# Attention on one core: eight pairs instead of ten transposed by transfers, another order of groups, a warm-up of 24 short matmuls, and stores split late

## The chip, the core and the metric

The kernel runs on one core of a Trainium2 chip. The core has five engines that run side by side and wait for each other by semaphores: TensorE (PE; its weight loads are listed as PEld), VectorE (DVE), ScalarE (ACT), GpSimd (POOL) and SyncE (SP). SyncE and ScalarE issue the DMAs here; 16 DMA engines carry them out. The metric is the device time of one execution in microseconds.

## The reference

Plain softmax attention for 8 batches of 8 heads, 512 positions of 64 values each:

```python
def reference(q, k, v):
    scale = 1.0 / np.sqrt(q.shape[-1])
    scores = np.einsum('bhqd,bhkd->bhqk', q, k) * scale
    scores = scores - scores.max(axis=-1, keepdims=True)
    attn = np.exp(scores)
    attn = attn / attn.sum(axis=-1, keepdims=True)
    return np.einsum('bhqk,bhkd->bhqd', attn, v).astype(np.float32)
```

The kernel leaves the maximum out, takes exp(scores x scale) as it is, and gets the sum of each row as a 65th output column, from a column of ones beside v.

## The kernel before

**Work.** The 64 heads are 32 pairs, g = 0 to 31. Of a pair, the 512 keys are four blocks of 128 (c = 0 to 3), each for two heads: 8 blocks of 128 keys x 512 queries, 256 in all. Two blocks make a group, m, with one exponential of 128 x 1024; there are 128 groups and four to a pair (the last group is split into two halves). Three buffers of the accumulation memory hold scores, so the scores of group m wait until the exponential of an earlier group has read its buffer.

**Steps of a pair.** Three loads bring q, k and v in 32 bits (`load`). GpSimd converts them to 16 bits (`cast`): q and k into `qkp`, v into one of 12 tiles `vp`. q and k must be transposed into `tqk`. For most pairs TensorE does so (`transposes`, 8 matmuls against an identity, and `copy`, one VectorE copy of 128 x 1024). For the pairs in `FLIPPED` a transposing DMA does so, from `qkp` to `tqk` without TensorE and VectorE (`flip`). Then come the scores (`scores`, two matmuls per group, one for each head, on separate halves of the rows), the exponential, and the output (`values`: for each 128 queries of a head, called a unit, four matmuls of 65 columns accumulate over the key blocks). Seven units share one bank of the accumulation memory; VectorE takes the reciprocals of their sums and multiplies (`recip`, `norm`, `mult`) into a ring of 56 units, from which SyncE stores (`Stores`). There are two such banks (`x0`, `x1`), which the transposes use too.

**Who exponentiates.** ScalarE does 115 groups. For the 13 groups in `ON_DVE`, VectorE computes the exponential by a polynomial: TensorE first adds a constant by two matmuls (`lift`), then VectorE runs `raise_` and three passes over 128 x 1024. For the groups in `SHARED`, GpSimd computes the middle one of the three. In most of them the scores' buffer is free after the second pass; in those of `SHARED` and `FREED` it is after the first.

**Order.** `Plan` walks through a model of the kernel in steps of 5 ns, with a cost for each kind of step, and writes a list of steps; the kernel then issues the instructions in the order of that list, and each engine takes its own in that order. So a constant of `Plan` moves no work by itself: it changes where in each engine's queue a step stands. `LATE_NORM`, `LATE_MULT` and `LATE_COPY` say how long a ready normalisation or copy may be held back for a pass; `ROOM` when a normalisation is taken in two parts; `SLACK` how far behind a VectorE group's last pass its block counts as there. A DMA in SyncE's queue waits for its data, and for the landing of an earlier DMA whose semaphore it reuses; everything behind it waits too.

**Stores.** `Stores.ready` gives a store of both heads of a pair (256 KB) where they lie side by side in the ring, and of one head (128 KB) otherwise. The last head is apart: its output comes in two halves of two units (`last_values`, `finish`), the first stored by SyncE, the second by ScalarE's queue.

**Start.** Pair 0 is written out by hand (`first_pair`): TensorE multiplies ones by ones (`busy`) until q is there, then transposes in pieces, with more such matmuls in the gaps, and the first three groups go through four exponentials (L846). The others are L650.

Of the kernel before, what the change touches and what calls it, by code (L numbers as in the profile page):

```python
# [16 lines left out]

class Stores:

    def __init__(self, pairs, units):  # L20
        self.pairs, self.units = pairs, units
        self.started = []
        self.waiting = []
# [5 lines left out]
    def ready(self, upto):  # L29

        found = []
        while self.waiting and self.waiting[0][2] + 4 <= upto:
            g, h, u = self.waiting[0]
            n = 1
            if h == 0 and u % self.units + 8 <= self.units:
                if len(self.waiting) > 1:
                    if self.waiting[1][0] == g:
                        n = 2
                elif g < self.pairs - 1 and (g, 1 - h) not in self.started:
                    break  # L40
            if u + 4 * n > upto:
                break
            found.append(self.waiting[:n])
            del self.waiting[:n]
        return found

class Plan:
# [7 lines left out]
    COPY_1 = (400, 190)  # L56
    NORM_COLUMN, PASS_DONE = 67, 80
    RECIP, RECIP_DONE, CHAINED = 80, 230, 117
    APART, ROOM = 1, 1200
    PASS, PASSES = 1131, 3  # L60
    OFFSET = 216
    FIRST_EXP = 5130
    STEP = 5
    CALM, KEEN = 14000, 7
    FIRST_UNIT, FIRST_VALUES = 4, 6000
    ON_DVE = (8, 16, 29, 36, 48, 53, 65, 74, 82, 90, 97, 104, 112)
    SHARED = (48, 90, 104)
    FREED = (36, 97, 112)

    LATE_NORM, LATE_MULT, LATE_COPY, HURRY, SOON, BACKLOG = 1000, 1300, 1000, 800, 80, 1500  # L70
    SLACK, AHEAD = 300, 2

    CAST, CAST_DONE, TO_POOL = 560, 130, 150
    SCALED, MORE = 595, 75
    MIDDLE, MIDDLE_DONE = (1120, 2300), 250
    FIRST_LAND, LOAD, STORE, LATENCY, ISSUE, FLIP_ISSUE = 5200, 700, 350, 2300, 540, 1490
    RAW, QK16, NV = 7, 5, 12
    FLIPPED = (22, 23, 24, 25, 26, 27, 28, 29, 30, 31)
    LEAD, FLIP = 8000, 3500
    RING = 56  # L80

    def __init__(self, groups, pairs, first):
# [27 lines left out]

        late = {grp[0][0] for m, grp in enumerate(groups) if m in self.ON_DVE}
        due = []
        for g in range(pairs):
            scores = 5000 + 3380 * g
            if g:
                lead = self.LEAD if g in self.FLIPPED else 2300
                due += [(scores - lead, g, "k"), (scores - lead + 10, g, "q")]
# [3 lines left out]
        self.extra = {}  # L121
        for m in self.ON_DVE:
            g = groups[m][0][0]
# [15 lines left out]
    def released(self, m):  # L139
        return 0 if m in self.SHARED or m in self.FREED else 1  # L140

# [3 lines left out]
    def emit(self, t, after):  # L145
# [3 lines left out]
        if not shared:  # L149
            self.casts.append((g, n, t if after is None else after + self.TO_POOL))  # L150
        if n == "q" and g in self.FLIPPED:
            self.note(t, "flip", g)
# [65 lines left out]
    def for_dve(self, m):  # L218
        return m in self.ON_DVE

# [29 lines left out]
    def transposes(self, t):  # L250
# [6 lines left out]
        if self.part_t == 2:  # L257
            self.transposed[self.next_t] = self.pe + self.TO_DVE
            self.ready.append((self.pe + self.TO_DVE, "copy", (self.next_t, self.bank_t)))
            self.next_t += 1  # L260
            while self.next_t in self.FLIPPED:
                self.next_t += 1
# [92 lines left out]
    def step_dve(self, t):  # L355
# [56 lines left out]
        elif any(x[2] <= t for x in self.passes):  # L412
# [5 lines left out]
            if all(x[0] > end - late[x[1]] for x in self.ready):  # L418
# [11 lines left out]
                del self.passes[after]  # L430
                if s == 0 and m in self.SHARED:
                    self.passes.remove((m, 1, 1e9))
# [24 lines left out]
def kernel(  # L457
# [7 lines left out]
    nc = tc.nc  # L465
    B, H, S, D = q.shape
    P = 128
# [6 lines left out]
    LAST = NP - 1  # L474
# [11 lines left out]
    raises = {}  # L486
    for m in Plan.ON_DVE:
        (g, c, _), (g2, c2, _) = groups[m]
# [35 lines left out]
    def source(src, g):  # L524
        b, h = g // ppb, 2 * (g % ppb)
        return src[b, h : h + 2].rearrange("h (p i) d -> p h i d", i=NI)
# [151 lines left out]
    def pass_(m, s):  # L678
# [7 lines left out]
        last = s == 2  # L686
        shared = m in Plan.SHARED
        one = low if m not in Plan.FREED else f
        dve(
# [78 lines left out]
    def finish(half):  # L768
        o = last[half]
        n = slice(2 * half, 2 * half + 2)  # L770
        ob = opool.tile([P, 2, D], FP32, tag="obl", name=f"obl_{half}")
        rc = opool.tile([P, 7, 1], FP32, tag="rc", name=f"rc_last_{half}")
        nc.vector.reciprocal(out=rc[:, 0:2], in_=o[:, :, D : D + 1])  # L773
        nc.vector.tensor_tensor(  # L774
            out=ob[:, :, :],
            in0=o[:, :, 0:D],
            in1=rc[:, 0:2].broadcast_to([P, 2, D]),
            op=AluOp.mult,
        )
        queue = (nc.sync, nc.scalar)[half]  # L780
        queue.dma_start(out=source(out, LAST)[:, 1, n], in_=ob[:, :, :])

    def first_loads():
        tk = load_tile(0, "k")
# [11 lines left out]
    def busy(dst, n):  # L796

        nc.tensor.matmul(dst[:, 0:n], ones[:, 0:P], ones[:, 0:n], start=True, stop=True)  # L798

    def first_pair():  # L800

        tk, tq = raw[0]["k"], raw[0]["q"]
        k16 = cpool.tile([P, 2, NI, D], FP16, name="k16_0")
        q16 = cpool.tile([P, 2, NI, 2, D], FP16, name="q16_0")
        kt = cpool.tile([P, 2, 2, P], FP16, name="kt_0")
        qt = cpool.tile([P, 2, NI, P], FP16, name="qt_0")

        def twice(h, i, n):
            return tq[:, h, i : i + n].rearrange("p i (x d) -> p i x d", x=1).broadcast_to([P, n, 2, D])  # L810

        nc.vector.tensor_copy(out=q16[:, 0, 0:2], in_=twice(0, 0, 2))
        nc.vector.tensor_copy(out=k16[:, 0, 0:2], in_=tk[:, 0, 0:2])
        nc.vector.tensor_copy(out=q16[:, 0, 2:4], in_=twice(0, 2, 2))
        nc.scalar.copy(k16[:, 0, 2:4], tk[:, 0, 2:4])
        nc.gpsimd.tensor_copy(out=q16[:, 1, 0:2], in_=twice(1, 0, 2))
        nc.gpsimd.tensor_copy(out=k16[:, 1, 2:4], in_=tk[:, 1, 2:4])

        pka, st1, st0 = (buffer(b, f"st_{n}") for b, n in enumerate(("ka", "1", "0a")))
        pqa = ps_x.tile([P, 8, P], FP16, tag="x0", name="tp_qa")  # L820
        pqb = ps_x.tile([P, 8, P], FP16, tag="x1", name="tp_qb")

        pka, pkc, pqc = pka[:, 0, :], st1[:, 0, :], st1[:, 1, :]
        pka, pkc, pqc = (
            t.bitcast(FP16).rearrange("p (n c) -> p n c", c=P) for t in (pka, pkc, pqc)
        )

        def t_k(dst, h, j):
            nc.tensor.transpose(
                dst, k16[:, h, 2 * j : 2 * j + 2, :].rearrange("p i d -> p (i d)"), ident  # L830
            )

        def t_q(dst, h, i):
            nc.tensor.transpose(dst, q16[:, h, i].rearrange("p x d -> p (x d)"), ident)  # L834

        def first_scores(st, h, j, q0, q1, pt, s0, s1):
            for x in range(2):
                s = slice(64 * x, 64 * x + 64)
                nc.tensor.matmul(  # L839
                    st[:, x, s0:s1],  # L840
                    kt[s, h, j, :],
                    qt[s, h].rearrange("p i c -> p (i c)")[:, q0:q1],
                    start=True,
                    stop=True,
                )
            nc.scalar.activation(  # L846
                out=pt[:, :, q0:q1], in_=st[:, :, s0:s1], func=EXP, scale=scale
            )

        for n in (512, 512, 512, 512, 512, 256):  # L850
            busy(st0[:, 0], n)
        for i in range(2):
            t_q(pqa[:, i], 0, i)
        t_k(pka[:, 0], 0, 0)
        busy(st0[:, 0], 2 * P)
        for i in range(2):
            t_q(pqc[:, i], 0, 2 + i)
        t_k(pkc[:, 0], 0, 1)
        nc.vector.tensor_copy(out=qt[:, 0, 0:2], in_=pqa[:, 0:2])
        nc.vector.tensor_copy(out=kt[:, 0, 0], in_=pka[:, 0])  # L860
        nc.vector.tensor_copy(out=qt[:, 0, 2:4], in_=pqc[:, 0:2])
        nc.vector.tensor_copy(out=kt[:, 0, 1], in_=pkc[:, 0])
        nc.vector.tensor_copy(out=q16[:, 1, 2:4], in_=twice(1, 2, 2))
        nc.vector.tensor_copy(out=k16[:, 1, 0:2], in_=tk[:, 1, 0:2])
        busy(st0[:, 1], 2 * P)
        pts = [ppool.tile([P, 2, S], FP16, tag="pt", name=f"pt_{m}") for m in range(3)]
        for m in range(3):
            for x, b in enumerate(groups[m]):
                blocks[b] = pts[m][:, x, :]
        first_scores(st0, 0, 0, 0, 256, pts[0], 0, 256)  # L870
        st0b = buffer(0, "st_0b")
        busy(st0b[:, 0, 256:512], P)
        first_scores(st0b, 0, 0, 256, 512, pts[0], 0, 256)
        first_scores(st1, 0, 1, 0, S, pts[1], 0, S)
        for i in (2, 3, 0, 1):
            t_q(pqb[:, i], 1, i)
        nc.vector.tensor_copy(out=qt[:, 1], in_=pqb[:, 0:4])  # L877
        pkb = ps_x.tile([P, 8, P], FP16, tag="x0", name="tp_kb")
        for j in range(2):
            t_k(pkb[:, j], 1, j)  # L880
        nc.vector.tensor_copy(out=kt[:, 1, 0], in_=pkb[:, 0])
        st2 = buffer(2, "st_2")
        busy(st2[:, 0], 3 * P)
        first_scores(st2, 1, 0, 0, S, pts[2], 0, S)
        nc.vector.tensor_copy(out=kt[:, 1, 1], in_=pkb[:, 1])
        first.update(kt=kt, qt=qt)
# [64 lines left out]
```

## Time and profile before

| | |
|---|---|
| three timed runs | 119.07, 116.71, 116.79 us (median 116.79) |
| the profiled execution | 116.59 us, its span 114.8 us |
| TensorE, matmuls | busy 103.4 us (90%), 1500 |
| VectorE | busy 100.3 us (87%), 179 instructions |
| ScalarE | busy 107.4 us (94%), 119 |
| GpSimd | busy 73.3 us (64%), 121 |
| DMA | 36.43 MB, mean 317 GB/s; 379 to 386 GB/s in most slices up to 50 us |
| the chain that ended last | ScalarE 70%, TensorE 17% |

A line of the profile's groups names the source line, the engine, the operation, the tile written and the tiles read, how many, then busy time and mean ns of one, then the idle time of the engine just before them and what ended most of it. In the timeline and the chain a line begins with its start and its length in us; `x8` says that eight instructions are merged in it. The span counts from the first instruction of the program to the last; the time of an execution is longer by what the profile does not cover. An instruction's duration can hold time in which it stood in line behind the one before it, so the pace of a row of equal instructions is read from their starts.

VectorE's and TensorE's busy shares over stretches of the span, in us:

| stretch | TensorE | VectorE | ScalarE | GpSimd |
|---|---|---|---|---|
| 10 to 25 | 13.75 | 13.72 | 15.00 | 11.15 |
| 25 to 40 | 13.61 | 13.92 | 15.00 | 11.45 |
| 40 to 55 | 14.56 | 14.56 | 15.00 | 10.90 |
| 55 to 70 | 14.11 | 14.71 | 15.00 | 11.53 |
| 70 to 80 | 9.73 | 9.93 | 10.00 | 6.30 |
| 80 to 90 | 9.86 | 9.73 | 10.00 | 7.98 |
| 90 to 100 | 9.34 | 9.74 | 10.00 | 7.23 |
| 100 to 110 | 9.22 | 7.59 | 10.00 | 1.51 |

### The profile page before, as it was taken

The numbers are of one execution on the slowest core, as the hardware profiler recorded it, in microseconds if no ns is written. First come the engines' busy times: TensorE is split into PE (matmuls) and PEld (weight loads), VectorE is DVE, ScalarE is ACT, GpSimd is POOL, SyncE is SP. The second block draws the span as 40 slices with busy tenths as digits, with TensorE's granted clock in tenths as the row PEclk, the third lists the DMA queues.
The fourth block names the chain that finished last, engine by engine and source line by source line (L and its number), as shares of the span: only waits on it lengthen the run. The fifth ranks groups of instructions, "written<-read, shape, count | busy, mean of one in ns | idle before, by whom it ended". The sixth has DMA issues, their size and how long they took to land.

```text
span 114.8 us, 3911 instructions
## 1 busy us (share of the span) xinstructions
PE 103.4 (90%) x1500; PEld 63.4 (55%) x1500; DVE 100.3 (87%) x179; ACT 107.4 (94%) x119; POOL 73.3 (64%) x121
## 2 busy tenths in 40 slices
PE   7979999798998999999898999999999989979970
PEld 2435564465563565666564566555667555547650
DVE  4653799996999999999999999999999999997480
ACT  4399999999999999999999999999999999999970
POOL 2289845969995629994779496593995557922000
PEclk9999999999999999999999999999999999999999
DMA  3899999999999999999999999989999999997452
GB/s 97 265 367 380 384 379 380 386 379 379 383 382 381 377 384 385 374 383 381 357 364 379 375 285 332 313 252 352 226 320 327 135 332 329 197 339 244 135 184 90
DMA packets 45795, 36.43 MB, mean 317 GB/s; under 512 B 12752, under 2 KB 45776, under 8 KB 45776
## 3 DMA queue, kind: packets, MB, share of 16 engines
q1 hardware_dynamic: 45344, 35.86, 101.0%
q10 hardware_dynamic: 432, 0.33, 0.9%
q8 instruction: 11, 0.18, 0.6%
q14 instruction: 8, 0.07, 0.2%
HBM read 25.17 MB, written 8.39 MB: 292 GB/s over the span
## 4 chain that ended last, share of the span: by engine, by line
ACT 70%; PE 17%; issue 7%; DMA 2%; DVE 2%; ACTq 0%
ACT pt L650 69%; PE st L645 7%; PE o L743 6%; DMA q<-in_q_dram 2%; ACT pt L846 1%; PE st L839 1%; DVE obl L774 1%; PE st_0a L798 0%; DVE qt L877 0%; PE tp_qa L834 0%; DVE rc_last L773 0%; PE tp_qb L834 0%; PE tp L593 0%; PE st_0b L839 0%; PE st_0a L839 0%
## 5 line engine op out<-in xcount | busy, mean ns | idle before, releaser
L650 ACT ACTIVATE pt<-st 128x1024 f16<-128x1024 f32 (+1 forms) x113 | 102.8, 1204 | 0.0
L645 PE MATMUL st<-tqk 64*128 64x512 f16 (+1 forms) x250 | 47.5, 380 | 6.1 <-ACT pt L650 4.6
L743 PE MATMUL o<-vp,pt 128*128 128x65 f16 x904 | 44.6, 195 | 0.2 <-ACT pt L650 0.2
L743 PEld LDWEIGHTS <-pt 128*128 128x128 f16 x904 | 36.2, 98 | 15.6 <-issue 14.4
L551 POOL CAST vp<-v 128x512 f16<-128x512 f32 x32 | 19.6, 619 | 8.8 <-PE o L743 2.4
L645 PEld LDWEIGHTS <-tqk 64*128 64x128 f16 x250 | 14.1, 93 | 17.8 <-issue 9.3
L568 POOL CAST qkp<-k 128x512 f16<-128x512 f32 x31 | 19.0, 614 | 7.0 <-DVE y L690 1.7
L719 DVE TENSOR_TENSOR ring<-o,rc 128x448 f32<-128x448 f32 (+2 forms) x37 | 22.4, 607 | 0.8
L568 POOL CAST qkp<-q 128x512 f16<-128x512 f32 x30 | 18.5, 616 | 6.8 <-DVE pd L690 2.9
L668 DVE TENSOR_SCALAR z<-st 128x1024 f32<-128x1024 f32 x13 | 15.7, 1206 | 0.9 <-PE st L645 0.9
L743 PE MATMUL o<-vp,pd 128*128 128x65 f16 x104 | 16.2, 195 | 0.1
L690 DVE SCALAR_TENSOR_TENSOR pd<-y,z 128x1024 uint32<-128x1024 f32 x13 | 16.0, 1229 | 0.0
L690 DVE SCALAR_TENSOR_TENSOR y<-st,z 128x1024 f32<-128x1024 uint16 x13 | 15.6, 1203 | 0.1
L613 DVE COPY tqk<-tp 128x1024 f16<-128x1024 f16 x20 | 13.6, 680 | 2.1 <-PE tp L593 1.9
L593 PE MATMUL tp<-ident,qkp 128*128 128x128 f16 x168 | 13.7, 220 | 0.1
L593 PEld LDWEIGHTS <-qkp 128*128 128x128 f16 x168 | 9.6, 98 | 5.8 <-issue 3.2
L743 PEld LDWEIGHTS <-pd 128*128 128x128 f16 x104 | 10.2, 98 | 3.0 <-issue 2.6
L711 DVE RECIPROCAL rc<-o 128x7 f32<-128x7 f32 (+2 forms) x37 | 7.3, 197 | 3.8 <-PE o L743 3.6
L567 POOL TENSOR_SCALAR k<-k 128x128 f32<-128x128 f32 x13 | 6.9, 530 | 4.4 <-PE st L645 2.6
L690 DVE SCALAR_TENSOR_TENSOR y<-st,y 128x1024 f32<-128x1024 uint16 x7 | 8.5, 1208 | 0.0
L706 POOL TENSOR_TENSOR y<-t,y 128x1024 f32<-128x1024 f32 x3 | 7.1, 2369 | 0.2
L631 PE MATMUL st<-const-bfloat16-1.0,lift 64*128 64x512 bf16 x26 | 5.0, 379 | 0.0
(57 smaller groups left out, 34.4 us busy)
## 6 DMA issues: line engine op xcount, KB each, us to landing
v<-in_v_dram SPq DMA_DIRECT2D x32, 256.0 KB, 5.4
k<-in_k_dram SPq DMA_DIRECT2D x31, 256.0 KB, 5.4
q<-in_q_dram SPq DMA_DIRECT2D x31, 256.0 KB, 5.4
out_dram<-ring SPq DMA_DIRECT2D x27, 256.0 KB, 4.4
out_dram<-ring SPq DMA_DIRECT2D x9, 128.0 KB, 4.3
tqk<-qkp SPq DMA_TRANSPOSE x10, 5.3
k<-in_k_dram ACTq DMA_DIRECT2D x1, 128.0 KB, 2.6
q<-in_q_dram SPq DMA_DIRECT2D x2, 64.0 KB, 2.3
```

The source lines that it names most:

```text
L551: return nc.gpsimd.tensor_copy(out=vps[g % NV][:, :, :, 0:D], in_=raw[g]["v"][:, :, :, :])
L568: ins = nc.gpsimd.tensor_copy(out=dst, in_=src[:, :, :, :])
L593: nc.tensor.transpose(tps[g][:, n, i, :], qkp[g][:, n, i, :], ident)
L613: nc.vector.tensor_copy(out=tqk[g][:, :, :], in_=tps.pop(g).rearrange("p n i c -> p n (i c)"))
L645: nc.tensor.matmul(st[:, x, cols], kc, qc[:, cols], start=not on_dve, stop=True)
L650: nc.scalar.activation(out=pt[:, :, cols], in_=st[:, :, cols], func=EXP, scale=scale)
L668: nc.vector.tensor_scalar(out=r["z"][:, :, :], in0=r["st"][:, :, :], scalar1=128.0, scalar2=2.0**17, op0=AluOp.mult, op1=AluOp.max,)
L690: nc.vector.scalar_tensor_tensor(out=r["bits"][:, :, :] if last else y, in0=(low, one, y)[s], scalar=(QUARTIC if shared else CUBIC)[s], in ...
L706: nc.gpsimd.tensor_tensor(out=y[:, :, :], in0=t[:, :, :], in1=y[:, :, :], op=AluOp.mult)
L711: dve(nc.vector.reciprocal(out=rcs[u][:, 0:n], in_=o[:, x : x + n, D : D + 1]))
L719: nc.vector.tensor_tensor(out=ring[:, u % NU : u % NU + n, :], in0=o[:, x : x + n, 0:D], in1=rc[:, 0:n].broadcast_to([P, n, D]), op=AluOp. ...
L743: nc.tensor.matmul(os[u // 7][:, u % 7, :], blocks[(g, c, h)][:, y * P : (y + 1) * P], vps[g % NV][:, h, c, :], start=(c == 0), stop=(c == ...
```

## The change

Pairs 22 and 23 are transposed by TensorE and not by a transfer. The 13 groups of VectorE are others (three of them shared with GpSimd as before, two instead of three in `FREED`), and four limits of the planner change; with them the order of nearly every engine changes from about group 18 on. From pair 25 on, the two heads of a pair are stored apart. Each of the last two stores is issued as two halves of 64 partitions, one on SyncE's queue and one on ScalarE's. The matmuls of ones at the start are cut into pieces of 128 columns: 24 first (five of 512 and one of 256 before), then 2, 2, 1 and 3 for 256, 256, 128 and 384 columns. There are 152 DMAs in place of 147: two transposing ones less, five stores of the ring and two of the last head more.

```diff
 class Stores:
+    MERGED = 25
...
-            if h == 0 and u % self.units + 8 <= self.units:
+            if h == 0 and g < self.MERGED and u % self.units + 8 <= self.units:
...
-    APART, ROOM = 1, 1200
+    APART, ROOM = 1, 2500
...
-    ON_DVE = (8, 16, 29, 36, 48, 53, 65, 74, 82, 90, 97, 104, 112)
-    SHARED = (48, 90, 104)
-    FREED = (36, 97, 112)
-
-    LATE_NORM, LATE_MULT, LATE_COPY, HURRY, SOON, BACKLOG = 1000, 1300, 1000, 800, 80, 1500
-    SLACK, AHEAD = 300, 2
+    ON_DVE = (8, 16, 26, 36, 44, 50, 62, 70, 79, 85, 96, 103, 111)
+    SHARED = (44, 79, 96)
+    FREED = (85, 103)
+
+    LATE_NORM, LATE_MULT, LATE_COPY, HURRY, SOON, BACKLOG = 1600, 1300, 2200, 800, 80, 1500
+    SLACK, AHEAD = 100, 2
...
-    FLIPPED = (22, 23, 24, 25, 26, 27, 28, 29, 30, 31)
+    FLIPPED = (24, 25, 26, 27, 28, 29, 30, 31)
...
-        queue = (nc.sync, nc.scalar)[half]
-        queue.dma_start(out=source(out, LAST)[:, 1, n], in_=ob[:, :, :])
+        for x, queue in enumerate((nc.sync, nc.scalar)):
+            some = slice(64 * x, 64 * x + 64)
+            queue.dma_start(out=source(out, LAST)[some, 1, n], in_=ob[some, :, :])
...
-        for n in (512, 512, 512, 512, 512, 256):
-            busy(st0[:, 0], n)
+        for _ in range(24):
+            busy(st0[:, 0], P)
...
-        busy(st0[:, 0], 2 * P)
+        for n in range(2):
+            busy(st0[:, 0], P)
...
-        busy(st0[:, 1], 2 * P)
+        for n in range(2):
+            busy(st0[:, 1], P)
...
-        busy(st0b[:, 0, 256:512], P)
+        for n in range(1):
+            busy(st0b[:, 0, 256:512], P)
...
-        busy(st2[:, 0], 3 * P)
+        for n in range(3):
+            busy(st2[:, 0], P)
```

## The prediction

> **What bounds the kernel now.** I read the groups of instructions first, then the list for the line of the exponentials, the chain of waits at both ends, and the timeline of the DMA queue.
>
> ```profile
> L650 ACT ACTIVATE pt<-st 128x1024 f16<-128x1024 f32 (+1 forms) x113 | 102.8, 1204 | 0.0
> ...
> L650 ACT ACTIVATE pt<-st x113: 722/1227/1321, 8.3 to 110.4; 128x1024 f16<-128x1024 f32 x111, 128x512 f16<-128x512 f32 x2
> ```
>
> The last column of the first line is ScalarE's idle time before these instructions: 0.0. The second gives first and last start. Between them lie 111 full exponentials and one half, so (110.4 - 8.3 - 0.5) / 111 = 0.915 us for each (0.5: the half, which the chain starts at 109.95). I call 0.915 us a slot. ScalarE never waits for 102 us, so nothing that is sped up in the middle can show; only work ahead of 8.3 us, work behind the last exponential, or a new hole in ScalarE's row can.
>
> ```profile
> 3.46 0.40 PE tp_qa L834 x2
> ...
> 3.97 0.21 PE st_0a L798
> 4.18 0.21 PE st L834 x2
> ...
> 6.00 0.34 PE tp_qb L834 x4
> 6.34 0.03 issue
> 6.37 0.42 DVE qt L877
> 6.79 0.14 DVE kt L881
> 6.93 0.05 issue
> 6.98 0.41 PE st L839 x2
> 7.38 0.02 issue
> 7.41 1.02 ACT pt L846
> 8.43 24.33 ACT pt L650 x27
> ```
>
> Start, length, what: the chain before the steady state starts when the first q and its cast are there (3.46) and runs over TensorE, VectorE, TensorE. Two matmuls of 128 columns take 0.21 us at 4.18; the eight of one tile at 7.51 take 0.62 from first start to last end, 0.22 being one alone, so 0.057 each. TensorE goes at half pace until shortly before 5.9 us, though the page's clock row shows 9 throughout. The fourth exponential starts 0.27 us after ScalarE fell idle.
>
> ```profile
> 110.72 0.31 PE o_last L759 x4
> ...
> 111.75 0.29 DVE obl L774
> ...
> 112.08 0.35 ACTq L781 DMA_DIRECT2D out_dram<-obl  x1
> ```
>
> The tail: the last store is issued at 112.08 and SyncE waits 1.7 us for its landing (until 113.7); 1.1 us of closing work follows.
>
> ```profile
> 85.88 1.39 SPq L599 DMA_TRANSPOSE tqk<-qkp  x1
> ...
> 96.05 2.51 SPq L599 DMA_TRANSPOSE tqk<-qkp  x1
> ...
> 99.29 1.28 SPq L599 DMA_TRANSPOSE tqk<-qkp  x1
> ...
> DMA to landing us min/median/max: 3.3/5.3/6.5
> ```
>
> These transposing transfers (pairs 27, 30, 31; the last line is over all ten) are the one supply with little to spare. The scores of pair 27 begin on TensorE at 92.81, 6.9 us behind the issue; of pair 30 at 102.51, 6.5 behind; of pair 31 at 106.52, 7.2 behind. At the median landing, 1.2 to 1.9 us are over.
>
> **The change part by part.** The sum is made against the profiled execution: 116.59 us, a span of 114.8 and 1.8 around it. The three timed runs have 116.71, 116.79 and 119.07, so it stands 0.2 below their median.
>
> *Warm-up.* Out go five matmuls of 512 columns and one of 256 (2,816 columns, 0.76 to 3.06 at 0.427 us per 512); in come 24 of 128 (3,072 columns). At 0.107 each, the pace of the cold 128-column matmuls, 24 take 2.56 us and end their streaming at 3.32, ahead of 3.46, when the first q is ready. Cover 0.14 us, cost 0. That each loads its own weights (0.147 us, the median of that line) costs nothing where loads overlap: the transposes at 3.97 to 4.29 each load their own and still come every 0.107. The other splits (two, two, one and three of 128) keep their columns. I take 0; the ends are +3.4 and -0.6, both rivals below.
>
> The Trainium skill, "TensorE: Matmul & The Clock Gate", section "Part 3: Packing small matmuls", says that a weight load overlaps running matmuls only if it is for another row group. By that rule 24 loads at the page's 107 ns would stand in line with 24 matmuls, 5.1 us instead of 2.56. This trace disagrees: full-height transposes, one row group, come every 0.107 us with a load each.
>
> *Two more pairs transposed on TensorE* (22 and 23): 16 matmuls of 0.057, 0.9 us, and two copies of 0.68 on VectorE, 1.36 us. They lie beside ScalarE's exponentials. VectorE is busy 14.71 of 15 us between 55 and 70 and 9.93 of 10 between 70 and 80, so its cover is only order: the passes of the groups that it exponentiates can slide, their blocks being read slots later. If nothing slid, normalisations would come late, then the banks they free, then TensorE's output matmuls: up to 1.36. SyncE loses two issues of 1.47 us (median). I take 0.
>
> *New places of the thirteen VectorE groups, and the new waiting limits.* Same number of groups, raises, passes (36) and middle steps (3): no work is added, only order. From the orders of both programs I counted TensorE's work between score groups, at 0.038 us per output matmul (16 in 0.61), 0.32 per score pair, 0.06 per transpose, 0.22 per lift pair. The densest 12 groups were 46 to 57: 9.67 us against ten slots on ScalarE (two groups are VectorE's), 9.15, a debt of 0.5 that ScalarE's row did not show. Now it is 91 to 102, 180 output matmuls, 12 score pairs and a lift pair: 10.9 us against eleven slots, 10.07, a debt of 0.8. The excess of 0.3 over what is shown to be covered is the upper bound; the lower is 0 (ScalarE cannot go faster than its slot). I take 0, nearest to the row of before. The slack that the plan keeps behind a VectorE group's last pass falls from 0.3 to 0.1 us, so TensorE can come to an unfinished block and hold back the scores queued behind it: in the old order it waited so once, 0.3 us, and nothing showed; 0 again, with 0.2 as the end.
>
> *Later flips.* In the list of steps the q cast of pair 30 stood 15 score groups ahead of that pair's first; now 8. Pair 31: 17, now 8. Pair 27: 21, now 10. Eight groups are 7.3 us; less about half a slot for the place within it and 0.62 for the cast, 6.2 us are left from a possible issue to the use. Before, the casts were early and SyncE was late (its queue ran without a gap of 0.5 us from 85 to 101), so the issue came 6.5 to 7.2 us ahead. So the spare time shrinks from 1.2 to 0.9 us at the median landing (5.3), and is -0.3 at the longest (6.5). The last three landed in 3.3 to 4.9 us. Cost: 0, with 0.3 per late transfer as its end, 0.7 if the issue slips a store (0.4) as well.
>
> *Stores.* From pair 25 on each head goes alone: five issues more on SyncE, 0.37 us each, past flips 27 to 31 and past the last store. The two flips that went pay for them. At the very end two single stores must go between 110.13 and 111.06, where one went: 2 x 0.42 = 0.84 against 0.93. They fit by 0.1 us; cost 0, and if they did not, the queue's next item (111.06) would slide by what is over.
>
> *The last two stores in halves on two queues.* Each half issues 32 KB. 64 KB took 1.5 to 1.6 us to landing; the first 64 KB loads 2.3 against 2.6 for 128 KB, 0.3 per 64 KB. Half of that is 0.15; some of it is not in series, so -0.1, between -0.2 and 0. The second issue on each queue waits for the first (0.35 us from 111.58: over at 111.93, before 112.08).
>
> Sum: 116.59 + 0 + 0 + 0 - 0.1 = 116.5 us.
>
> **The rivals.**
> - *The clock opens earlier.* TensorE's denser warm-up, 0.26 us longer, could bring full pace before 3.46 instead of before 5.9. Then the first exponential could come about 0.25 sooner (half of the streaming on its path), and the fourth 0.37 sooner still (7.41 against 6.12 + 0.92). Up to -0.6: 115.9. For it: the half pace is in the rows. Against: TensorE's first 2.5 us are as busy as before. The Trainium skill, "TensorE: Matmul & The Clock Gate", section "Part 1: The HAM clock gate", puts the opening at the end of a busy window of 3.4 us that runs free of the kernel; by that rule the two kernels would differ only by where the window lies, and no run here shows that yet. Chance 0.15.
> - *A hole in ScalarE's row* (slower than before): the flip of pair 30 or 31 lands after TensorE has come to its scores, and everything queued behind those scores on TensorE waits too. It decides when issue to landing exceeds 6.2 us, which one of ten did (6.5). Price 0.3 to 0.75, and with TensorE's debt of 0.3 beside it up to 1.0, as ScalarE cannot catch up: 116.8 to 117.6. For it: the halved lead, VectorE without slack. Against: late transfers landed fastest, and fewer flips run. Chance 0.2, of which 0.03 for several holes that sum to over 2.3 us.
> - *Weight loads in series*: 24 x (0.147 + 0.107) = 6.1 us, the first transpose at 6.86 in place of 3.46, +3.4: 119.9. Against it the 0.107 rows. Chance 0.02.
> - *The halved last stores do nothing*, 116.6: inside the forecast.
>
> **How the numbers follow.** The forecast, 116.5 (116.2 to 116.8 by itself), has 0.63. The range takes the early clock in (115.9) and most holes (to 117.3); outside stay the serial loads and the worst holes, some 0.1. Two per cent, 2.3 us, is about what a measurement of this kernel can tell from no change. Faster by that much needs more than -0.6 and -0.2 give: 0.01. Slower: 0.03 + 0.02 = 0.05. Within: 0.94.
>
> **What would show it.** The row of exponentials keeps idle 0.0 and 0.915 us per slot; its first start stays at 8.3 (7.7 with the early clock, 11.7 with serial loads); TensorE's 24 matmuls end before 3.5; eight flips land before the first scores of their pairs; the wait for the last store is 1.6. I am wrong if that row shows idle time, if the wait named for scores is a flip, or if the span ends more than 1.1 us behind the last landing.

## The result, and the profile after

| | before | after |
|---|---|---|
| median | 116.75 us (22 runs) | 117.69 us (22 runs) |
| the profiled execution | 116.59 us, span 114.8 us | 117.33 us, span 115.5 us |

The ratio of the times is 1.0064, with a 95% interval of 1.0043 to 1.0085. The change costs about 0.75 us: inside two per cent, but clear of zero, and above the range that was forecast. The ratio leaves out executions that stand over 1.5 per cent above the fastest of their kernel, so it is smaller than that of the two medians.

Four lines of the page after stand first: busy times and counts, one DMA queue, the chain's shares, and the group of the exponentials.

```profile
PE 104.6 (91%) x1538; PEld 66.9 (58%) x1538; DVE 101.0 (87%) x181; ACT 107.5 (93%) x119; POOL 73.6 (64%) x121
...
q8 instruction: 12, 0.20, 0.6%
...
ACT 46%; PE 37%; DVE 10%; issue 4%; ACTq 0%
...
L652 ACT ACTIVATE pt<-st 128x1024 f16<-128x1024 f32 (+1 forms) x113 | 102.9, 1148 | 0.0
```

The exponentials still have 0.0 us of idle time ahead of them, as in the kernel before, so the middle is as it was. The line of queue 8 is easily passed over. Its columns are packets, MB and share; on the page before it reads:

```profile
q8 instruction: 11, 0.18, 0.6%
```

The list for the line of the exponentials (count, shortest, median and longest ns, first and last start), and then the list for the transposing transfers, of the kernel after:

```profile
L652 ACT ACTIVATE pt<-st x113: 678/1158/1305, 8.5 to 110.7; 128x1024 f16<-128x1024 f32 x111, 128x512 f16<-128x512 f32 x2
```

```profile
L601 SPq DMA_TRANSPOSE tqk<-qkp x8: 1238/1293/2235, 71.2 to 100.0; - x8
...
DMA to landing us min/median/max: 2.8/4.7/6.0
```

From first to last start it is again (110.7 - 8.5 - 0.5) / 111 = 0.916 us a slot, with the half taken off as before. The eight transfers landed 2.1 us or more before TensorE came to their pair's first scores (before: 1.1 us or more, for pair 27).

The chain of waits at the start of the kernel after:

```profile
0.76 2.72 PE st_0a L801 x24
3.47 0.30 PE tp_qa L837 x2
...
7.12 0.41 PE st L842 x2
7.53 0.02 issue
7.55 1.02 ACT pt L849
8.58 1.83 ACT pt L652 x2
```

In the chain the 24 short matmuls are over at 3.47. By the trace the last of them starts at 3.16, and the first transpose at 3.38, 0.06 us behind the end of q's cast; before it was 3.46, also 0.06 behind that end. So the short matmuls hold up nothing. The chain's later steps stand 0.15 us later than before, at most.

The timeline of the last microseconds, after and then before (start, length, what; `x5` is five instructions merged):

```profile
107.49 3.88 ACT L652 ACTIVATE pt<-st 128x1024 f16<-128x1024 f32 x5
...
109.45 2.67 SPq L736 DMA_DIRECT2D out_dram<-ring  x5
...
111.80 1.18 ACTq L784 DMA_DIRECT2D out_dram<-obl  x2
...
112.21 1.19 SPq L784 DMA_DIRECT2D out_dram<-obl  x2
```

```profile
108.14 3.02 ACT L650 ACTIVATE pt<-st 128x1024 f16<-128x1024 f32 x4
...
109.23 2.17 SPq L734 DMA_DIRECT2D out_dram<-ring  x3
...
111.58 0.34 SPq L781 DMA_DIRECT2D out_dram<-obl  x1
...
112.08 0.35 ACTq L781 DMA_DIRECT2D out_dram<-obl  x1
```

ScalarE ends at 111.37 (107.49 + 3.88) instead of 111.16, 0.21 us later. But the last issue is over at 113.40 (112.21 + 1.19) instead of 112.43, 0.97 later. I call the time from ScalarE's last end to the landing of the last store the *tail*: 2.51 us before, 3.32 after. The DMA view of the same stretches gives the stores of the last head (KB each, median us from issue to landing), after and before:

```profile
out_dram<-obl ACTq DMA_DIRECT2D x2, 32.0 KB, 1.9
out_dram<-obl SPq DMA_DIRECT2D x2, 32.0 KB, 1.8
```

```profile
out_dram<-obl SPq DMA_DIRECT2D x1, 64.0 KB, 1.5
out_dram<-obl ACTq DMA_DIRECT2D x1, 64.0 KB, 1.6
```

Half the bytes take longer to land, not less. The two profiled executions differ by 0.74 us: first exponential +0.15, from there to ScalarE's last end +0.07, tail +0.82, from the last landing to the end of the span -0.30 (1.14 to 0.85). So the loss is in the tail. Two suspects stand there: the halves, and the twelfth packet of queue 8, which starts 2.0 us ahead of ScalarE's end (at 109.35).

### The profile page after: what moved, and what is told of

It is laid out like the page before. It is cut to its first block, busy times and chain, and to the rows that moved or that the text cites. A ratio compares the mean times of both kernels' runs of the same rounds, so it can differ in the third digit from the quotient of the medians.

```text
span 115.5 us, 4009 instructions
## 1 busy us (share of the span) xinstructions
PE 104.6 (91%) x1538; PEld 66.9 (58%) x1538; DVE 101.0 (87%) x181; ACT 107.5 (93%) x119; POOL 73.6 (64%) x121
## 4 chain that ended last, share of the span: by engine, by line
ACT 46%; PE 37%; DVE 10%; issue 4%; ACTq 0%
ACT pt L652 45%; PE o L745 14%; PE st L647 13%; DVE y L692 3%; PE st_0a L801 3%; PE tp L595 3%; DVE z L670 2%; DVE tqk L615 2%; DVE pd L692 1%; PE st L633 1%; DVE ring L721 1%; ACT pt L849 1%; PE st L842 1%; DVE obl L776 1%; PE tp_qb L837 0%
## 5 line engine op out<-in xcount | busy, mean ns | idle before, releaser
L647 PE MATMUL st<-tqk 64*128 64x512 f16 (+1 forms) x250 | 47.0, 380 | 5.0 <-ACT pt L652 3.1
L745 PE MATMUL o<-vp,pt 128*128 128x65 f16 x904 | 43.9, 194 | 0.4 <-DVE tqk L615 0.3
L647 PEld LDWEIGHTS <-tqk 64*128 64x128 f16 x250 | 14.7, 93 | 17.1 <-issue 7.7
L615 DVE COPY tqk<-tp 128x1024 f16<-128x1024 f16 x22 | 14.8, 677 | 1.7 <-PE tp L595 1.7
L595 PE MATMUL tp<-ident,qkp 128*128 128x128 f16 x184 | 15.4, 220 | 0.2
L595 PEld LDWEIGHTS <-qkp 128*128 128x128 f16 x184 | 10.6, 97 | 7.0 <-issue 4.8
L692 DVE SCALAR_TENSOR_TENSOR y<-st,y 128x1024 f32<-128x1024 uint16 x8 | 9.7, 1212 | 0.0
```

The lines of the kernel that those rows point to most:

```text
L595: nc.tensor.transpose(tps[g][:, n, i, :], qkp[g][:, n, i, :], ident)
L615: nc.vector.tensor_copy(out=tqk[g][:, :, :], in_=tps.pop(g).rearrange("p n i c -> p n (i c)"))
L647: nc.tensor.matmul(st[:, x, cols], kc, qc[:, cols], start=not on_dve, stop=True)
L692: nc.vector.scalar_tensor_tensor(out=r["bits"][:, :, :] if last else y, in0=(low, one, y)[s], scalar=(QUARTIC if shared else CUBIC)[s], in ...
L745: nc.tensor.matmul(os[u // 7][:, u % 7, :], blocks[(g, c, h)][:, y * P : (y + 1) * P], vps[g % NV][:, h, c, :], start=(c == 0), stop=(c == ...
```

## The experiments

All comparisons are with the kernel before, run on the same chip. A kernel's edit is against the kernel before where nothing else is said.

**First: each part by itself.**

`e1_warmup`, the short matmuls of the start alone:

```diff
-        for n in (512, 512, 512, 512, 512, 256):
-            busy(st0[:, 0], n)
+        for _ in range(24):
+            busy(st0[:, 0], P)
```

(and the 2, 2, 1 and 3 pieces behind it).

> The kernel before with the 24 short matmuls of ones alone. Theory of the tail (the split stores at the end cost what the change costs): no change, ratio 1.000, within 0.002. Rival of the start (the short warm-up keeps TensorE at half pace longer, or holds up the first transposes): +0.3 to +0.8 us, ratio 1.003 to 1.007, and the 24 matmuls are the chain's piece ahead of the first transpose. Rival of the order: ratio 1.000.

Measured: 1.0071 [1.0028, 1.0113], so the theory that this would cost nothing is refuted. The number is the one that the rival of the start named, but not for its reason: the last short matmul starts at 3.16, ahead of the end of q's cast (3.31), and ScalarE's last end is only 0.13 us later than before, while the tail is 3.30 us, 0.79 longer. Page and timeline of this kernel:

```profile
q8 instruction: 12, 0.20, 0.6%
```

```profile
109.37 2.17 SPq L734 DMA_DIRECT2D out_dram<-ring  x3
...
111.72 0.98 SPq L781 DMA_DIRECT2D out_dram<-obl  x1
...
112.21 0.35 ACTq L781 DMA_DIRECT2D out_dram<-obl  x1
```

A change of the first 3 us made one issue of the last 4 us take 0.98 us instead of 0.34. The twelfth packet of queue 8 is the only new thing that I found there: it starts at 111.44 and takes 0.88 us. That issue ends 0.4 us behind it.

`e2_order`, the order alone: the new `ON_DVE`, `SHARED`, `FREED` and limits and eight flipped pairs, with the long warm-up, both heads in one store and whole last stores.

> The new order of groups and the eight flips, with the long warm-up, the ring stores merged as before and the last stores whole. Theory of the tail: +0.1 us at most, ratio 1.000 to 1.001, ScalarE's holes as in the changed kernel's trace (0.05 and 0.02 us). Rival of the order (holes in ScalarE's row that this one trace shows small, but other executions larger): +0.5 to +0.8 us, ratio 1.004 to 1.007.

Measured: 1.0041 [1.0014, 1.0069], again the number of the rival. But in its profile ScalarE's row, from the first start of the steady exponentials to the last end, is only 0.24 us longer than before (103.07 against 102.83). It has a twelfth packet as well, 0.30 us ahead of ScalarE's last end; its tail is 3.11 us, 0.60 longer.

`e3_last_halves`:

```diff
-        queue.dma_start(out=source(out, LAST)[:, 1, n], in_=ob[:, :, :])
+        for x, queue in enumerate((nc.sync, nc.scalar)):
+            some = slice(64 * x, 64 * x + 64)
+            queue.dma_start(out=source(out, LAST)[some, 1, n], in_=ob[some, :, :])
```

> The kernel before, with the last two stores in halves on both queues. Theory of the tail: two queues that issue at once take 0.53 to 0.56 us each in place of 0.35, so the last landing comes 0.3 to 0.5 us later behind the last exponential (2.50 us before): ratio 1.003 to 1.004. Prediction on record: -0.1 us, ratio 0.999.

Measured: 1.0100 [1.0063, 1.0137], tail 3.19 us, with eleven packets up to the end. Its timeline:

```profile
111.37 1.18 SPq L782 DMA_DIRECT2D out_dram<-obl  x2
111.37 1.45 ACTq L782 DMA_DIRECT2D out_dram<-obl  x2
```

Four issues take 0.56, 0.55, 0.53 and 0.81 us in place of two of 0.35. The first half-pair starts where the first whole store started (0.43 us behind ScalarE's end), but the second has to wait for it, until 1.08 instead of 0.92.

`e4_stores_apart`:

```diff
-            if h == 0 and u % self.units + 8 <= self.units:
+            if h == 0 and g < self.merged and u % self.units + 8 <= self.units:
...
+    stores.merged = 25
```

> The kernel before, with the ring stores from pair 25 on issued for each head alone; order of steps as before. Theory of the tail: SyncE comes 0.5 us late to its last store, but ScalarE's queue holds the one that ends last, so +0.1 to +0.2 us, ratio 1.001 to 1.002. If the stores alone make the tail: +0.5, ratio 1.004.

Measured: 0.9964 [0.9935, 0.9993], below all that was expected, tail 2.47 us. Timeline:

```profile
108.78 2.29 SPq L735 DMA_DIRECT2D out_dram<-ring  x5
...
111.16 0.40 SPq L782 DMA_DIRECT2D out_dram<-obl  x1
111.62 0.35 ACTq L782 DMA_DIRECT2D out_dram<-obl  x1
```

The two single stores do fit ahead of the first last store: five issues in 2.29 us, and the next starts 0.46 behind ScalarE's end (before: 0.42).

So two parts cost, 0.7 and 1.0 per cent, and together they cost 0.6. The costs don't add.

**Second: is it the packet, or the short matmuls themselves?** `f1_before_22_more` leaves the start alone and adds 22 matmuls that nothing reads, so that TensorE has as many instructions as in `e1_warmup`; `f2_warmup_16_more` adds 16 such ones to `e1_warmup`.

```diff
+    EXTRA = (17, 18, 19, 20, 21, 22, 23, 24, 25, 26, 27, 28, 30, 31, 32, 33, 34, 35, 37, 38, 39, 40)
...
+            if x == 0 and m in EXTRA:
+                nc.tensor.matmul(st[:, x, 0:P], kc, qc[:, 0:P], start=True, stop=True)
```

> The kernel before with 22 more small matmuls on TensorE in groups 17 to 40 (128 columns, overwritten at once by the scores): as many TensorE instructions as with the short warm-up, and the long warm-up kept. Theory of the code block (TensorE's instructions come in 16 KB blocks by DMA, one per some 256; more instructions bring a twelfth block, which lands among the last stores): the block starts within 0.5 us of the last exponential's end, the last landing moves from 2.5 to 3.0 to 3.4 us behind it, ratio 1.004 to 1.008. Rival (the warm-up itself was what cost 0.7%): ratio 0.999 to 1.002.

Measured: 1.0079 [1.0034, 1.0124]. With the old warm-up, the same tail returned (3.29 us), and so did the same issue, in the timeline:

```profile
111.23 0.97 SPq L785 DMA_DIRECT2D out_dram<-obl  x1
111.73 0.35 ACTq L785 DMA_DIRECT2D out_dram<-obl  x1
```

The packet starts 0.13 us behind ScalarE's end (`e1_warmup`: 0.15). Beside it ScalarE's row is 0.36 us longer than before, so the ratio is not the packet's alone; the issue and the tail are.

> The short warm-up on the kernel before, with 16 more small matmuls on TensorE in groups 17 to 34, so that it has as many TensorE instructions as the changed kernel. Theory of the code block: the twelfth block moves 32 instructions forward, to 109.4 us as in the changed kernel, ahead of the last stores; the last landing is back at 2.5 to 2.8 us behind the last exponential, ratio 0.999 to 1.003. Rival (the warm-up costs by itself): 1.006 to 1.008 as with the warm-up alone.

Measured: 1.0042 [0.9998, 1.0085], which tells little. The tail did not come back to 2.5 to 2.8 us as expected: the packet moved only to 0.71 us ahead of ScalarE's end (some 2 were expected), among the issues, one of which took 1.28 us. The tail was 3.63, and ScalarE's row 0.64 us longer than before.

**Third: the changed kernel with one part undone.** `f3_changed_last_whole` has the last two stores whole; `f4_changed_merged` has `MERGED` at 32, so the two heads of a pair go together again.

> The changed kernel with the last two stores whole, as before. Theory of the tail: the last landing comes 2.5 to 2.7 us behind the last exponential in place of 3.32; ratio to the kernel before 1.001 to 1.003. Rival of the order and the start: ratio stays at 1.006.

Measured: 0.9948 [0.9907, 0.9989], against 1.0064 with the halves. Tail 2.90 us (after: 3.32). The ratio is below what was expected, the tail above it. In its timeline something is still wrong with the stores of the ring:

```profile
108.44 2.99 SPq L736 DMA_DIRECT2D out_dram<-ring  x5
...
111.28 0.35 ACTq L783 DMA_DIRECT2D out_dram<-obl  x1
111.52 0.39 SPq L783 DMA_DIRECT2D out_dram<-obl  x1
```

Five issues take 2.99 us (`e4_stores_apart`: 2.29), one of them 1.15: it started 0.42 us behind the start of the twelfth packet and ended 0.39 behind its end. SyncE's last store slides to 1.16 us behind ScalarE's end.

> The changed kernel with the ring stores merged as before, the last stores in halves. Theory of the tail: SyncE comes to the last halves 0.4 us earlier, but the halves still take 0.53 to 0.56 us each to issue: last landing 3.0 to 3.2 us behind the last exponential, ratio to before 1.004 to 1.006. If the stores apart were the cause: 2.5 us and 1.001.

Measured: 1.0015 [0.9981, 1.0049], tail 3.23 us. The tail is the one that the theory named, the ratio the one of its rival; the tail decides here, as the rival had it at 2.5. Here the packet (1.98 us ahead of ScalarE's end) holds up no issue by more than 0.05 us: the one that started 0.05 us behind it took 0.38, as before, and the next starts as it ends and takes 0.42 (before: 0.37). The tail is that of the halves alone.

**Fourth: sizes of both.** `g1_twelve_of_256` has a warm-up of 12 matmuls of 256 columns, six matmuls more than before instead of 22. `g2_halves_one_queue` gives both halves of a last store to one queue. `g3_no_halves_long_warmup` is `f3_changed_last_whole` with the long warm-up of before.

```diff
-        for x, queue in enumerate((nc.sync, nc.scalar)):
+        queue = (nc.sync, nc.scalar)[half]
+        for x in range(2):
             some = slice(64 * x, 64 * x + 64)
```

(`g2_halves_one_queue`, against `e3_last_halves`.)

> [...] Theory of the code block: too few for a twelfth block before the end of the work, last landing 2.5 us behind the last exponential, ratio 0.998 to 1.002. Rival (the longer warm-up itself, 256 columns more): 1.005 to 1.008.

Measured: 1.0037 [1.0003, 1.0071]. No twelfth packet up to the end of the span, and the tail is 2.50 us as before, with issues as before in its timeline:

```profile
112.01 0.34 SPq L781 DMA_DIRECT2D out_dram<-obl  x1
...
112.50 0.35 ACTq L781 DMA_DIRECT2D out_dram<-obl  x1
```

The profiled execution (118.24 us, far above this kernel's median of 116.97) had 0.7 us of idle time before exponentials and 3.0 us behind its span instead of 1.8, so only its tail is read here. The ratio lies between that of before and that of `e1_warmup` and decides nothing by itself.

> The kernel before, with each of the last two stores in two halves of 64 partitions, but both on one queue: the first on SyncE's, the second on ScalarE's. If it is two queues issuing at once that makes an issue 0.55 us long: issues back at 0.35, the last one starts 0.4 us later than the whole store did, last landing 2.8 to 2.9 us behind the last exponential, ratio 1.002 to 1.004. If it is the form with 64 partitions: issues of 0.53 to 0.56 here too, last landing 3.0 to 3.2, ratio 1.005 to 1.008.

Measured: 1.0146 [1.0086, 1.0206], tail 3.42 us, from two views:

```profile
112.06 1.19 SPq L783 DMA_DIRECT2D out_dram<-obl  x2
...
112.55 1.20 ACTq L783 DMA_DIRECT2D out_dram<-obl  x2
```

```profile
out_dram<-obl SPq DMA_DIRECT2D x2, 32.0 KB, 1.9
out_dram<-obl ACTq DMA_DIRECT2D x2, 32.0 KB, 1.9
```

SyncE's first half took 0.56 us to issue, while ScalarE's queue issued nothing for all but its last 0.06 us. So the long issue belongs to the half itself, not to two queues that issue at once. Tail and ratio are above what was expected; the kernel has six executions only.

> The changed kernel with the last two stores whole and with the long warm-up: new order, eight flips and stores apart remain. Theory of the code block: 44 TensorE instructions fewer than with the short warm-up move the twelfth block from 2.0 us ahead of the last exponential's end to about 0.3 ahead of it, among the last stores: last landing 3.0 to 3.4 us behind it, ratio 1.002 to 1.006, slower than the changed kernel with whole last stores (2.90 us, 0.995). Rival (the short warm-up costs by itself): faster than that kernel, 0.990 to 0.993.

Measured: 1.0041 [1.0012, 1.0069]. Taking the short matmuls out again did not help: TensorE has fewer instructions, so the packet comes later, 0.57 us ahead of ScalarE's end, and meets an issue of the ring (1.32 us). Tail 3.07. Timeline and DMA view of this kernel:

```profile
108.81 3.16 SPq L736 DMA_DIRECT2D out_dram<-ring  x5
```

```profile
q8 instruction: 1, 0.02, 2.3%
...
out_dram<-ring SPq DMA_DIRECT2D x5, 128.0 KB, 2.8
```

**Fifth: move the packet out of the way.** `h1_block_earlier` is `f3_changed_last_whole` with 16 unread matmuls, at earlier groups than in the second set:

```diff
+    EXTRA = (4, 5, 6, 10, 11, 12, 13, 14, 18, 19, 20, 21, 22, 23, 24, 28)
```

> The changed kernel with the last two stores whole, as in f3_changed_last_whole, and with 16 more small matmuls of TensorE that nothing reads (128 columns, ahead of the scores of 16 groups between 4 and 28), so that the program's twelfth 16 KB block of TensorE instructions is fetched earlier. It came 1.96 us ahead of ScalarE's last end with 3078 instructions and 0.57 ahead with 3034, 0.032 us for each, so with 3110 it should start about 3.0 us ahead, between SyncE's issues at -4.0 and -1.9. Theory (the place of the block makes the tail): no issue at the end takes over 0.5 us, and the tail from ScalarE's last end to the last landing is 2.5 to 2.6 us in place of 2.90; ratio to the kernel before 0.990 to 0.995 if the added matmuls make no hole in ScalarE's row, and their holes are read and taken off if they do. Rival (the stores apart and the new order make the tail of 2.9, whatever the block does): tail 2.9 to 3.1, ratio 0.995 to 1.000.

Measured: 0.9978 [0.9953, 1.0003]; median 116.30 us against 116.69. The packet runs from 2.55 to 1.60 us ahead of ScalarE's end (a start at 3.0 was expected). One issue starts while it runs, the first of the five below, and it takes 0.33 us as in `e4_stores_apart`; none is held up. Tail 2.48 us, as the theory had it. Timeline and DMA view:

```profile
108.51 2.29 SPq L740 DMA_DIRECT2D out_dram<-ring  x5
...
110.89 0.40 SPq L787 DMA_DIRECT2D out_dram<-obl  x1
111.35 0.35 ACTq L787 DMA_DIRECT2D out_dram<-obl  x1
```

```profile
q8 instruction: 1, 0.02, 1.7%
...
out_dram<-ring SPq DMA_DIRECT2D x5, 128.0 KB, 1.8
```

The same five stores take 2.29 us to issue instead of 3.16 in `g3_no_halves_long_warmup` (2.99 in `f3_changed_last_whole`), and 1.8 us to land instead of 2.8. The ratio missed what was expected (0.990 to 0.995): the 0.42 us that the tail lost against `f3_changed_last_whole` is not seen between the ratios of the two, whose intervals overlap.

**All of it in one table.** TensorE: matmuls on the page, each with a weight load. Packet: start of the twelfth, from ScalarE's last end. Tails are of one execution each.

| kernel | TensorE | packet, us | last stores | tail, us | ratio |
|---|---|---|---|---|---|
| before | 1500 | none | whole | 2.51 | 1 |
| `e4_stores_apart` | 1500 | none | whole | 2.47 | 0.9964 |
| `g1_twelve_of_256` | 1506 | none | whole | 2.50 | 1.0037 |
| `h1_block_earlier` | 1554 | -2.55 | whole | 2.48 | 0.9978 |
| `f3_changed_last_whole` | 1538 | -1.96 | whole | 2.90 | 0.9948 |
| `g3_no_halves_long_warmup` | 1516 | -0.57 | whole | 3.07 | 1.0041 |
| `e2_order` | 1516 | -0.30 | whole | 3.11 | 1.0041 |
| `e1_warmup` | 1522 | 0.15 | whole | 3.30 | 1.0071 |
| `f1_before_22_more` | 1522 | 0.13 | whole | 3.29 | 1.0079 |
| `f2_warmup_16_more` | 1538 | -0.71 | whole | 3.63 | 1.0042 |
| `e3_last_halves` | 1500 | none | halves | 3.19 | 1.0100 |
| `g2_halves_one_queue` | 1500 | none | halves | 3.42 | 1.0146 |
| `f4_changed_merged` | 1538 | -1.98 | halves | 3.23 | 1.0015 |
| after | 1538 | -2.02 | halves | 3.32 | 1.0064 |

Every kernel with whole last stores and no issue that the packet holds up has a tail of 2.5 us; every other has 2.9 to 3.6. From after to `f3_changed_last_whole` to `h1_block_earlier` the tail falls by 0.42 us for the halves and 0.42 for the packet, and is back at 2.48: together 0.84, against 0.82 lost. The shares depend on the order, though. `f4_changed_merged`, with halves and no issue held up, has 3.23, so beside the halves the packet and the single stores add only 0.10. Three ratios are below 1: those of `e4_stores_apart` and `f3_changed_last_whole` clear of noise, that of `h1_block_earlier` (0.9978) not.

The tails are of one execution each, but the record has the span of every execution of these runs. By the mean span over the executions that the ratios count, each kernel stands against the one before, in us, with standard errors of 0.1 to 0.2: `e1_warmup` +1.23, `e3_last_halves` +1.07, `f1_before_22_more` +1.05, `g2_halves_one_queue` +1.04, `f2_warmup_16_more` +0.70, `e2_order` +0.58, `g3_no_halves_long_warmup` +0.54, `f4_changed_merged` +0.45; `g1_twelve_of_256` +0.15, `f3_changed_last_whole` -0.13, `e4_stores_apart` -0.18, `h1_block_earlier` -0.22. So the kernels with a tail of 2.5 us are apart from those with a longer one, but for `f3_changed_last_whole`, whose longer tail its spans don't show.

The time behind the span is not the same for all, and the tails don't hold it. Mostly it is 1.7 to 2.1 us. In the kernels with eleven packets in the span (before, `e3_last_halves`, `e4_stores_apart`, `g1_twelve_of_256`, `g2_halves_one_queue`) it is 2.2 to 3.3 us in 25 of 150 executions, in those with twelve in none of 115. Two of the 25 were profiled, one of `e3_last_halves` (118.50 us) and one of `g1_twelve_of_256` (118.24): in both a twelfth packet starts at 117.5, behind the span's end at 115.2, and in the profiles of the other three kernels there is none. So some part of the ratios of `e3_last_halves`, `g1_twelve_of_256` and `g2_halves_one_queue` lies behind the span, and the packet that a kernel is spared in its tail can still come after it.

## Why the prediction was wrong

**The halved last stores: the step that failed.** The step "Half of that is 0.15; some of it is not in series, so -0.1, between -0.2 and 0" had the wrong sign, and its size lay outside its bounds. Measured: +0.42 us of tail where the halves are undone in the changed kernel, +0.69 alone (3.19 - 2.51). It took the price per KB from loads of 64 and 128 KB and went below them, as if landing were bytes. For stores of 32 KB the rows show 1.8 to 1.9 us in the median instead of 1.5 to 1.6, and issues of 0.53 to 0.60, twice 0.81, instead of 0.35. With "over at 111.93, before 112.08" it took the issue of a half as that of a whole store; at 0.55 the second half can't start when its data are there. Its rival "the halved last stores do nothing" was on the right side of it and not far enough. The rest of the miss is small: the sum was made against 116.59 us, 0.16 below the median of the kernel before.

**A term put at nothing: what TensorE's added instructions cost.** "Warm-up ... I take 0" and "Two more pairs ... I take 0" are right on the engines that they looked at. But 22 and 16 more matmuls, each with its weight load, bring the program's twelfth packet of instructions in among the last stores. By the table it costs 0.42 us of tail in the changed kernel with whole last stores, and 0.6 to 1.1 where it comes later. The page before shows the price's only sign, `q8 instruction: 11`; I had not asked what one of those packets would meet.

**The single stores at the end.** "They fit by 0.1 us" holds without the packet (`e4_stores_apart`, `h1_block_earlier`: the next issue starts 0.46 behind ScalarE's end, against 0.42). With it one issue takes 0.83 instead of 0.4, and SyncE's first half starts at 0.84 behind ScalarE's end. The 0.1 was no margin for that.

**What held.** The order: 0.0 idle on the page, 0.916 us a slot, and ScalarE's row 0.07 us longer than before (102.90 against 102.83), though 0.24 in `e2_order`. The flips: pair 30 was issued 6.0 us ahead of its scores (forecast 6.2), but landed in 2.8, so 3.2 us were over; the rival of a late flip did not occur. The warm-up: over at 3.47 (forecast "before 3.5"), and its matmuls start every 0.107 us with a load each, so loads in series are refuted. The span's end: 0.85 us behind the last landing. The named sign "the wait for the last store is 1.6" was the one that failed: it was 0.9 us in three pieces (before: 1.7 in one), as SyncE was issuing halves until 1.3 us ahead of the last landing. That only two per cent can be told from no change was too cautious: the interval is 0.4 per cent wide.

**The early clock.** The traces show no effect of the change on it: over the 14 profiled executions the first steady exponential starts at 7.5 to 8.5 in the six kernels with 24 short matmuls and at 7.5 to 8.8 in the eight others (8.3 before, 8.5 after). But the start varies between executions by more than that rival claimed. The kernel after and `f3_changed_last_whole` are the same program up to the last stores; the busy times of one stretch, of the kernel after and then of `f3_changed_last_whole` (stretch, length, busy us and instructions of PE, PEld, DVE, ACT and POOL, then the granted clock, DMA share and GB/s), and then the list for the exponentials of the latter:

```profile
5.00:6.00 1.00, 1.00 (x7) 0.28 (x7) 0.30 (x2) 1.00 (x2) 0.35 (x1) 1.00 1.05 360
```

```profile
5.00:6.00 1.00, 0.90 (x11) 0.55 (x9) 0.71 (x4) 1.00 (x3) 0.62 (x2) 1.00 1.08 356
```

```profile
L652 ACT ACTIVATE pt<-st x113: 678/1158/1307, 7.5 to 109.7; 128x1024 f16<-128x1024 f32 x111, 128x512 f16<-128x512 f32 x2
```

TensorE gets through 7 matmuls in the one and 11 in the other. By the trace's clock records full pace begins at 6.4 us and at 3.6, and all of ScalarE's row stands 1.0 us earlier (7.5 and 8.5), more than the whole change. The Trainium skill, "TensorE: Matmul & The Clock Gate", section "Part 1: The HAM clock gate", says that the opening of the gate varies from run to run, as its window runs free of the kernel; these traces agree, with 3.6 to 7.1 us over the executions profiled (first exponential at 7.5 in the one, at 8.8 in the other).

**What stays open.** How much of the 0.75 us is the halves' and how much the packet's is known for tails of single executions alone, and there it depends on which is undone first. By time the halves cost 1.2 per cent (1.0064 against 0.9948, each against other executions of the kernel before), some 1.35 us, by the tail 0.42; the variation of the start is in each of these medians. Why a half takes longer to issue, why an issue waits for a packet of instructions, and why `e4_stores_apart` is faster than before although its tail is not shorter, was not found.

## What to carry to other kernels

Count the instructions that an edit adds, not only their time: on the page, an instruction queue with one packet more is a transfer more, and where it falls is as much a part of the order as any store. At the end of this kernel the issues decided, not the bytes: cut no last store into pieces below the size whose issue and landing the trace shows. Where the start of a kernel varies by a microsecond, compare its last microseconds with those of the other kernel counted from the same event, and not the whole span.

## What the runs showed of the hardware

- **Instruction packets.** One packet of 16 KB goes over queue 8 for about every 250 of TensorE's instructions (matmuls and weight loads). The twelfth starts when TensorE has begun 3,006 to 3,052 of them; the span holds 11 packets for 3,000 and 3,012 instructions (before, `g1_twelve_of_256`) and 12 for 3,032 and more. A packet takes 0.9 to 1.9 us. The Trainium skill, "Runtime: NRT & Kernel Launch", section "Instruction fetch mechanics", has the block of 16 KiB for 256 instructions, and the trace agrees; it calls the cost of crossing such a boundary mostly hidden, and at this kernel's end the tail shows 0.4 to 1.1 us of it.
- **Issues beside a packet.** Over all packets of the 14 traces, SyncE began to issue 49 stores while one ran. 41 of these issues ended 0.2 to 0.7 us behind the packet's end (all but two of them 0.35 to 0.43) and took 0.60 to 1.74 us. The other eight took 0.33 to 0.38; in each of them SyncE had begun to issue its previous DMA 0.73 us or more ahead of the packet's start. In the 41 it was 0.67 us or less, or the previous DMA was a transposing one (0.9 to 1.5 us ahead). At the end of the work seven kernels have one such issue, of 0.64 to 1.32 us. In `h1_block_earlier` the DMA before the issue beside the packet had gone out 1.5 us ahead of the packet, and nothing was held up. Stores in flight land later too: in `e1_warmup` one of the ring took 3.6 us, 2.2 before.
- **Small stores.** 64 partitions of the last store (32 KB) issue in 0.53 to 0.60 us, twice in 0.81, and land in 1.8 to 2.2, on one queue or two; 128 partitions (64 KB), where no issue is held up, in 0.34 to 0.40 and 1.55 to 1.63.
